# Last expert's first-half merge for all tiles at once, a tile-by-tile norm behind it, and late weights split in pieces

## The chip, the core and the metric

The kernel runs on one core of a Trainium2 chip. The metric is the device time of one launch in microseconds (us). Engines are named as the profile names them: PE (matrix products), DVE and ACT (elementwise work), POOL (a third elementwise engine that also issues some DMAs), SP (issues most DMAs).

## The reference

Two streams, a prompt of 256 tokens and a sample of 512, go separately through the same two layers of width 1024. Each layer adds an attention block and a mixture of 16 experts to the residual `x`; each expert chooses its own tokens, 2n/16 of a stream's n:

```python
def expert_choice_ffn(h, w_router, w_gate, w_up, w_down):
    ...
    aff = jax.nn.softmax(jnp.einsum('nd,de->ne', x, w_router).astype(jnp.float32), axis=-1)
    g, idx = lax.top_k(aff.T, cap)
    xe = x[idx]
    hid = jax.nn.silu(jnp.einsum('ecd,edf->ecf', xe, w_gate)) * jnp.einsum('ecd,edf->ecf', xe, w_up)
    ye = jnp.einsum('ecf,efd->ecd', hid, w_down) * g[..., None].astype(x.dtype)
    y = jnp.zeros_like(x).at[idx.reshape(-1)].add(ye.reshape(-1, d))
...
    for l in range(DEPTH):
        x = x + token_mixer(rmsnorm(x, norm1[l]), w_in[l], rpb[l], gain_na[l], gain_dil[l], w_out[l], slopes)
        x = x + expert_choice_ffn(rmsnorm(x, norm2[l]), w_router[l], w_gate[l], w_up[l], w_down[l])
    return rmsnorm(x, final_norm)
```

All values are fp32. `token_mixer` projects to q, k and v with `w_in`, attends, normalises each head and multiplies by `w_out`.

## The kernel before

The 768 tokens of both streams are six tiles of 128 rows. A product of two fp32 matrices is made as three products of rounded parts: every operand is split into `hi` (a rounding copy, on ACT) and `lo` (the operand minus `hi`, on DVE), and hi·hi, hi·lo and lo·hi are summed in PSUM. For the weights `Stream` does this: `prefetch` asks for a raw load, `convert` makes `hi` (L230) and `lo` (L231), and a load's turn comes as earlier buffers are freed. The experts of a layer use 192 loads of 128x2048 (1 MB), four for each of gate, up and down; the mixer's `w_in` comes in loads of 128x1024, two for each unit of its projection.

`experts` runs gate, up and down for one expert after another. The 96 chosen rows of an expert (64 of the sample, 32 of the prompt) are the stationary operand; a down product collects its two halves of 512 columns in the PSUM banks `av` and `o` (L366), then ACT scales them by the gate weight (L413) and POOL adds the rows to `xres` in DRAM by an indirect DMA (L414). The last expert, 15, is not scattered. The class `Ending` takes it into `x` by a product: `load` builds a 96x768 matrix `at` of ones and zeros (L539: six comparisons of an iota with the token numbers) and loads the residual as twelve pieces of 128x512 (L544); `scaled` makes hi and lo of one half of the expert's rows (L549, L550); `merge(t, b)` multiplies tile t's columns of `at` with half b (two products, L555), adds the result to `x` (L557) and sums squares (L558); `begin` multiplies the first half by the norm's gain (L562); `factor` makes 1/rms (L314 on DVE, then `pow` on POOL, L316); `normed` scales the begun half by it on ACT (L570) and makes the rest on DVE (L574).

This happens twice. At the seam between the layers, `Mixer.ended` runs `merge`, `factor` and `normed` per tile, stores `x` to `xres` (L701), `turn_rows` transposes the normed rows (L730; splits at L733, L734), and the first unit of `project`, "v", multiplies them with `w_in` (L827 to L829: 24 products a tile). At the end, `final` does the same without a projection and stores the output (L517). Between the first and the second half of the last down product, `merge(t, 0)` of tiles 0 to 3 is put in.

Each engine executes its instructions in program order. Around the seam that order comes from generators (`ended`, `turn_rows`, `project`), from which `Order` picks the next by estimated ready times of a `Clock`. `busy(n)` puts n dummy products of the identity with itself on PE.

## Time and profile before

| quantity | value |
|---|---|
| median of three runs | 2029.87 us (2029.84 to 2031.87) |
| profiled execution | 2031.46 us |
| its span in the trace | 2029.7 us |
| PE busy | 1974.6 us, 97% of the span |
| DVE, ACT, POOL busy | 78%, 67%, 11% |
| the seam in the trace | about 990 to 1044 us |
| the end in the trace | about 1997 us to the span's end |

Times in the trace count from the span's start. The profiled execution is 1.6 us above the median, and 1.76 us of it lie outside the span. A row of the timeline gives a start, a length, the engine, the line, what is written from what, and in brackets the idle time before it with what ended that; consecutive like instructions are one row. A matrix product shows its own length from start to end although the next begins before that: eleven products of 512 columns in 2.79 us are about 0.24 us each. "PEclk" is the granted clock as a share of the full 2.4 GHz; 0.50 is 1.2 GHz.

### The profile page before, as it was taken

How to read it: one execution, taken by the hardware profiler on the slowest of the kernel's cores; microseconds unless marked ns; L12 is line 12 of the kernel's file. 1: busy time of each engine (PE TensorE's matmuls, PEld its weight loads, DVE VectorE, ACT ScalarE, POOL GpSimd, SP SyncE). 2: the span in 40 equal slices, each digit the busy share in tenths (PEclk: the TensorE clock that was granted, in tenths of full speed). 3: DMA queues.
4: the chain of work that ended last, by engine and by line, in shares of the span. 5: the costliest groups of instructions: out<-in, count | busy, mean ns of one | idle time of the engine just before them, and what ended most of it. 6: DMA issues, size and time to landing. Idle time of an engine off the chain costs nothing.

```text
span 2029.7 us, 27925 instructions
## 1 busy us (share of the span) xinstructions
PE 1974.6 (97%) x10602; PEld 1551.6 (76%) x10602; DVE 1586.8 (78%) x1978; ACT 1349.9 (67%) x1743; POOL 217.3 (11%) x167
## 2 busy tenths in 40 slices
PE   7999999999999999999999999999899999999997
PEld 7899897886777777777689998978767777777774
DVE  5666667778888888888856666776788888888888
ACT  4666666437777777777646666654477777777775
POOL 3000000010101010101020000100110101011011
PEclk9999999999999999999999999999999999999999
DMA  6222124679999999999352212256799999999974
GB/s 229 85 79 81 58 77 174 234 261 367 376 394 375 398 380 396 380 389 351 121 189 74 97 58 77 69 184 253 292 354 392 387 382 398 377 398 376 398 275 143
DMA packets 96693, 526.67 MB, mean 259 GB/s; under 512 B 12112, under 2 KB 15440, under 8 KB 47408
## 3 DMA queue, kind: packets, MB, share of 16 engines
q1 hardware_dynamic: 82080, 489.20, 62.8%
q0 software_dynamic: 8992, 29.25, 5.7%
q10 hardware_dynamic: 5488, 6.45, 1.3%
q8 instruction: 83, 1.36, 0.3%
q14 instruction: 50, 0.41, 0.1%
HBM read 485.79 MB, written 32.77 MB: 255 GB/s over the span
## 4 chain that ended last, share of the span: by engine, by line
PE 89%; DVE 5%; ACT 3%; DMA 1%; issue 1%; POOL 0%; ACTq 0%; POOLq 0%; SPq 0%; DVEq 0%
PE pj L366 17%; PE s L366 17%; PE av L366 9%; PE o L366 8%; PE pj L1091 4%; PE pj L797 4%; PE pj L799 4%; PE pj L798 4%; PE tp L941 3%; PE pj L827 2%; PE pj L829 2%; PE pj L828 2%; PE tp L349 2%; PE s L1091 2%; PE s L908 2%; PE av L969 2%
## 5 line engine op out<-in xcount | busy, mean ns | idle before, releaser
L230 ACT ACTIVATE hi<-data 128x2048 fp32r<-128x2048 f32 (+1 forms) x170 | 289.5, 1703 | 61.3 <-PE s L366 24.6
L231 DVE TENSOR_TENSOR hi<-data,hi 128x2048 fp32r<-128x2048 f32 (+1 forms) x106 | 197.9, 1867 | 51.2 <-ACT hi L230 50.6
L366 PE MATMUL pj<-hi,parts 128*96 128x512 f32 x880 | 233.8, 393 | 2.8 <-DVE parts L352 2.3
L917 ACT ACTIVATE data<-data 128x256 f32<-128x256 f32 (+1 forms) x192 | 119.1, 621 | 155.5 <-DVE data L915 147.3
L366 PE MATMUL s<-turned_lo,parts 128*96 128x512 f32 x872 | 221.7, 393 | 0.0
L366 PEld LDWEIGHTS pj<-hi,parts 128*96 128x96 f32 x880 | 141.6, 161 | 64.8 <-DVE parts L352 3.2
L366 PEld LDWEIGHTS s<-turned_lo,parts 128*96 128x96 f32 x872 | 140.4, 161 | 60.7 <-DVE turned_lo L231 0.4
L797 PE MATMUL pj<-turned,hi 128*128 128x256 f32 (+1 forms) x512 | 178.4, 348 | 1.3 <-ACT heads L764 1.0
L366 PE MATMUL pj<-turned_lo,parts 128*96 128x512 f32 x656 | 178.9, 395 | 0.5 <-ACT parts L351 0.5
L230 ACT ACTIVATE hi<-heads 128x2048 fp32r<-128x2048 f32 x80 | 152.9, 1913 | 32.4 <-PE s L366 20.4
L799 PE MATMUL pj<-turned,hi 128*128 128x256 f32 (+1 forms) x512 | 172.5, 337 | 0.0
L798 PE MATMUL pj<-turned_lo,hi 128*128 128x256 f32 (+1 forms) x512 | 172.4, 337 | 0.0
L231 DVE TENSOR_TENSOR turned_lo<-data,hi 128x2048 fp32r<-128x2048 f32 x64 | 146.7, 2292 | 29.6 <-ACT hi L230 28.1
L366 PE MATMUL s<-hi,parts 128*96 128x512 f32 x664 | 169.0, 392 | 0.0
L231 DVE TENSOR_TENSOR turned_lo<-data,turned_lo 128x2048 fp32r<-128x2048 f32 (+1 forms) x68 | 151.4, 2226 | 16.8 <-ACT turned_lo L230 15.0
L414 POOL DMA_INDIRECT xres<-heads,iT x30 | 53.9, 1797 | 916.6 <-ACT heads L413 916.6
L230 ACT ACTIVATE turned_lo<-data 128x2048 fp32r<-128x2048 f32 (+1 forms) x68 | 127.0, 1868 | 27.8 <-PE pj L366 12.3
L366 PEld LDWEIGHTS s<-hi,parts 128*96 128x96 f32 x664 | 107.1, 161 | 46.3
L946 DVE TENSOR_TENSOR parts<-tp,parts 128x512 fp32r<-128x512 f32 (+2 forms) x160 | 99.6, 647 | 51.0 <-ACT parts L945 49.3
L366 PE MATMUL av<-hi,parts 128*96 128x512 f32 x400 | 134.9, 398 | 3.7 <-DVE hi L231 3.7
L366 PEld LDWEIGHTS pj<-turned_lo,parts 128*96 128x96 f32 x656 | 103.5, 162 | 42.3 <-ACT parts L351 0.9
L915 DVE CUSTOM_DVE_ANT_0 data<-s,data 128x512 f32<-128x512 f32 (+2 forms) x176 | 98.7, 579 | 28.8 <-PE s L909 27.1
(175 smaller groups left out, 4514.6 us busy)
## 6 DMA issues: line engine op xcount, KB each, us to landing
...
```

The costliest lines, as they stand in the source:

```text
L230: nc.scalar.activation(hi, w, AF.Copy)
L231: x = nc.vector.tensor_sub(lo, w, hi.bitcast(F32))
L366: nc.tensor.matmul(ps[b], y[:, k, :], a[:, o:o + 512], start=k == 0 and w == 0, stop=k == KT - 1 and w == 2)
L414: nc.gpsimd.indirect_dma_start(out=self.xres, out_offset=bass.IndirectOffsetOnAxis(ap=iT[:, e:e + 1], axis=0), in_=y, in_offset=None, comp ...
L797: nc.tensor.matmul(p, hi[:, k, :], hT[0][:, k, s], start=k == 0, stop=False)
L798: nc.tensor.matmul(p, hi[:, k, :], hT[1][:, k, s], start=False, stop=False)
L799: nc.tensor.matmul(p, lo[:, k, :], hT[0][:, k, s], start=False, stop=k == KT - 1)
L915: nc.vector.tensor_tensor_reduce(out=x[:, j, :w], in0=p[:, j, :w], in1=tab[:, o:o + w], scale=-1.0, scalar=3.0e38, op0=OP.add, op1=OP.min, ...
L917: nc.scalar.activation(x[:, j, :w], x[:, j, :w], AF.Exp, bias=m, scale=-1.0, accum_out=self.den[n][:, t, a:a + 1])
L941: nc.tensor.transpose(p[:, a * S + t * 128:a * S + (t + 1) * 128], w[:, o:o + 128], self.k.ident)
L946: nc.vector.tensor_sub(lo[:, c], p[:, c], hi[:, c].bitcast(F32))
L1091: nc.tensor.matmul(p, y[:, i], z[:, b * 512:(b + 1) * 512], start=i == 0 and w == 0, stop=i == len(ks) - 1 and w == 2)
```

## The change

The last three weight loads of each layer are converted in two pieces of 1024 columns. Expert 14's second half is scaled on DVE instead of ACT, and the conversions of these loads come right behind. The building of `at` moves from DVE to POOL. Between the halves of the last down product, the first half is multiplied for all six tiles (two use the `tp` banks), with adds of four tiles at the seam and all six at the end. The load of the first `w_in` part moves from POOL's DMA queue to SP's, and both parts are loaded ahead of the twelve `x` pieces and converted early, the second one's `lo` on POOL. `begin` covers two tiles instead of three at the seam, and six instead of four at the end, from tile 2 on by POOL. `ended` goes tile by tile in a fixed order, with dummy products between. The first layer's "v" unit waits for one weight part instead of two.

```diff
@@ class Stream, convert @@
+            pool = g in self.by_pool
+            n = size // self.pieces.get(g, 1)
+            for o in range(0, size, n):
+                c = slice(o, o + n)
...
-                nc.scalar.activation(hi, w, AF.Copy)
-                x = nc.vector.tensor_sub(lo, w, hi.bitcast(F32))
+                nc.scalar.activation(hi[:, c], w[:, c], AF.Copy)
+                x = (nc.gpsimd if pool else nc.vector).tensor_sub(lo[:, c], w[:, c], hi[:, c].bitcast(F32))
@@ experts @@
-            for b in range(2):
-                nc.scalar.activation(y[:, b * 512:(b + 1) * 512], dp[b], AF.Copy, scale=gT[:, e:e + 1])
+            nc.scalar.activation(y[:, :512], dp[0], AF.Copy, scale=gT[:, e:e + 1])
+            if e + 2 < EXPERTS:
+                nc.scalar.activation(y[:, 512:], dp[1], AF.Copy, scale=gT[:, e:e + 1])
+            else:
+                nc.vector.tensor_scalar_mul(y[:, 512:], dp[1], gT[:, e:e + 1])
+                ws.convert(stop - 2)
...
-        if m:
-            ws.prefetch(stop + 1, nc.gpsimd)
+        ws.prefetch(stop + 2)
         end.load()
         dp = acc("av", "o")
-        banks = {t: self.bank(("pj", "s")[t // 2]) for t in range(4)}
+        banks = {t: self.bank(("pj", "s", "tp")[t // 2]) for t in range(TILES)}
         for i in product(c, hT[last], dp, True):
             if i == 1:
                 end.scaled(0, dp[0])
+                ws.convert(min(stop + 1, len(ws.load)))
             if i == 2:
-                ws.prefetch(stop + 2)
-                for t in range(4):
-                    end.merge(t, 0, banks[t])
+                for t in range(TILES):
+                    end.multiply(t, 0, banks[t])
+                for t in range(4 if m else TILES):
+                    end.add(t, 0, banks[t])
+                    if t < 4:
+                        end.square(t, 0)
                 for t in range(end.early):
                     end.begin(t)
-                ws.convert(min(stop + 1, len(ws.load)))
         end.scaled(1, dp[1])
+        if m:
+            self.busy(BUSY[4])
+            end.add(4, 0, banks[4])
+            ws.convert(stop + 2)
+            end.rest = banks[5]
+        end.square(4, 0)
@@ expert_loads @@
+            if i >= len(src) - 3:
+                self.ws.pieces[n] = 2
@@ final @@
         def sums(t):
-            for b in range(t < 4, 2):
-                end.merge(t, b, self.bank(("pj", "s")[t % 2]))
+            end.merge(t, 1, self.bank(("pj", "s")[t % 2]))
@@ class Ending @@
-        self.early = 3 if m else 4
+        self.early = 2 if m else TILES
...
-            self.nc.vector.tensor_scalar(self.at[:, t * 128:(t + 1) * 128], self.k.iota, self.k.iL, -128.0 * t,
+            self.nc.gpsimd.tensor_scalar(self.at[:, t * 128:(t + 1) * 128], self.k.iota, self.k.iL, -128.0 * t,
...
-        self.nc.vector.tensor_mul(self.h[t][:, s], self.x[t][:, s], self.g[:, s])
+        (self.nc.vector if t < 2 else self.nc.gpsimd).tensor_mul(self.h[t][:, s], self.x[t][:, s], self.g[:, s])
@@ class Mixer, __init__ and ended @@
+        if l:
+            ws.by_pool.add(fi + 1)
...
+        merge(0)
+        busy(BUSY[5])
+        merge(1)
+        factor(0)
+        end.add(5, 0, end.rest)
+        merge(2)
+        busy(BUSY[6])
+        for t in range(TILES):
+            yield lambda: r_at[t] if self.turned >= t - 1 else NEVER
+            end.normed(t, rs[t])
+            if t == 0:
+                end.square(5, 0)
+            self.h_at[t] = clock.dve(512 if t < end.early else 1024, r_at[t])
+            if t + 1 < TILES:
+                factor(t + 1)
+            if t + 3 < TILES:
+                yield lambda: self.avail(("s", "pj")[(t + 3) // 2 % 2]) if self.turned > t else NEVER
+                merge(t + 3)
```

In the changed file the same lines have other numbers: L366 is L372, L555 is L575, L557 is L579, L562 is L592, L730 is L776, L827 is L882, L231 is L237, L549 and L550 are L569 and L570, and a dummy product is L311.

PE's program at the seam, before, from the last products of expert 15's first half (`av`) to the first product of the "v" unit (`pj<-hi,turned`); `parts` under L555 is the matrix `at`:

```order
L366 MATMUL av<-hi,parts 96x512 x13
L366 MATMUL o<-turned_lo,parts 96x512 x12
L555 MATMUL pj<-hi,parts 128x512 x4
L555 MATMUL s<-hi,parts 128x512 x4
...
L366 MATMUL o<-hi,parts 96x512
L555 MATMUL s<-hi,parts 128x512 x4
L555 MATMUL pj<-hi,parts 128x512 x4
L555 MATMUL s<-hi,parts 128x512 x4
L730 MATMUL tp<-ident,data 128x128 x8
L555 MATMUL s<-hi,parts 128x512 x4
L730 MATMUL tp<-ident,data 128x128 x8
L827 MATMUL pj<-hi,turned 128x256
```

The same place in the changed program, where `av<-ident` are the dummy products:

```order
L372 MATMUL av<-hi,parts 96x512 x13
L372 MATMUL o<-turned_lo,parts 96x512 x12
L575 MATMUL pj<-hi,parts 128x512 x4
L575 MATMUL s<-hi,parts 128x512 x4
L575 MATMUL tp<-hi,parts 128x512 x4
...
L311 MATMUL av<-ident 128x128 x5
L575 MATMUL s<-hi,parts 128x512 x2
L311 MATMUL av<-ident 128x128 x2
L575 MATMUL s<-hi,parts 128x512 x2
L575 MATMUL pj<-hi,parts 128x512 x2
L311 MATMUL av<-ident 128x128 x6
L776 MATMUL tp<-ident,data 128x128 x8
L575 MATMUL pj<-hi,parts 128x512 x2
L882 MATMUL pj<-hi,turned 128x256
```

All first-half merge products now stand between the halves of the down product; of the second-half ones eight stand ahead of the first "v" product instead of all, and the last two tiles' come between tiles of the "v" unit. The first "v" product follows one tile's transposes instead of two.

DVE's program at the seam, before, from expert 15's last split of hidden rows (L352) to the second scaled half:

```order
L352 TENSOR_TENSOR parts<-tp,parts 128x384 x2
L539 TENSOR_SCALAR parts<-iota,iL 96x128 x6
L231 TENSOR_TENSOR hi<-heads_3427,hi 128x2048
L231 TENSOR_TENSOR turned_lo<-heads_3711,turned_lo 128x2048
L231 TENSOR_TENSOR turned_lo<-turned,hi 128x2048
L550 SCALAR_TENSOR_TENSOR hi<-av,gT,hi 96x512
L557 TENSOR_TENSOR data<-data,pj 128x512 x2
L557 TENSOR_TENSOR data<-data,s 128x512 x2
L562 TENSOR_TENSOR data<-data 128x512 x3
L231 TENSOR_TENSOR hi<-data,hi 128x1024
L550 SCALAR_TENSOR_TENSOR hi<-o,gT,hi 96x512
```

And changed, where L422 is the scaling of expert 14's second half:

```order
L358 TENSOR_TENSOR parts<-tp,parts 128x384 x2
L422 TENSOR_SCALAR heads_3711<-o,gT 96x512
L237 TENSOR_TENSOR hi<-heads_3427,hi 128x1024 x2
L237 TENSOR_TENSOR turned_lo<-heads_3711,turned_lo 128x1024 x2
L237 TENSOR_TENSOR turned_lo<-turned,hi 128x1024 x2
L570 SCALAR_TENSOR_TENSOR hi<-av,gT,hi 96x512
L237 TENSOR_TENSOR hi<-data,hi 128x1024
L579 TENSOR_TENSOR data<-data,pj 128x512 x2
L579 TENSOR_TENSOR data<-data,s 128x512 x2
L592 TENSOR_TENSOR data<-data 128x512 x2
L570 SCALAR_TENSOR_TENSOR hi<-o,gT,hi 96x512
```

The six comparisons have left DVE, three conversions have become six, and the conversion of the first `w_in` part stands ahead of the adds instead of behind the `begin`s. On POOL, the end of the program changes from

```order
L339 DMA heads_11430<-table,iT 96x1024
L414 DMA xres<-heads_11430,iT 768x1024
L339 DMA heads_11430<-table,iT 96x1024
L414 DMA xres<-heads_11430,iT 768x1024 x2
L316 TENSOR_TENSOR data<-data,half 128x1 x6
```

to

```order
L345 DMA heads_11450<-table,iT 96x1024
L424 DMA xres<-heads_11450,iT 768x1024
L345 DMA heads_11450<-table,iT 96x1024
L424 DMA xres<-heads_11450,iT 768x1024 x2
L559 TENSOR_SCALAR parts<-iota,iL 96x128 x6
L592 TENSOR_TENSOR data<-data 128x512 x4
L322 TENSOR_TENSOR data<-data,half 128x1 x6
```

POOL now builds `at` and makes four of the begun halves (L592) ahead of the six `pow`s (L322). At the seam it builds `at` and makes the `lo` of the second `w_in` part ahead of them.

## Rows read from the trace of the kernel before

**Rows 1.** Page, part 1: busy time, share of the span and instructions of each engine

```profile
PE 1974.6 (97%) x10602; PEld 1551.6 (76%) x10602; DVE 1586.8 (78%) x1978; ACT 1349.9 (67%) x1743; POOL 217.3 (11%) x167
```

**Rows 2.** Stretches: length, PE busy (instructions), PEclk, DMA share, GB/s

```profile
994.00:997.00 3.00, 1.15 (x6) 0.96 1.02 180
997.00:1000.00 3.00, 3.00 (x9) 0.50 0.72 248
1008.00:1012.00 4.00, 2.36 (x6) 0.80 0.43 173
1020.00:1024.00 4.00, 3.35 (x16) 0.58 0.25 101
2001.00:2004.00 3.00, 2.42 (x11) 1.00 0.39 76
```

**Rows 3.** Timeline of PE, seam: start, length, operation, count, [idle, releaser]

```profile
995.90 4.29 PE L366 MATMUL av<-hi,parts 128*96 128x512 f32 x11 [1.85 <-DVE hi L231]
...
1002.85 1.09 PE L555 MATMUL pj<-hi,parts 96*128 96x512 f32 x4
...
1008.80 0.51 PE L555 MATMUL s<-hi,parts 96*128 96x512 f32 x1 [1.16 <-ACT hi L549]
...
1014.87 1.09 PE L730 MATMUL tp<-ident,data 128*128 128x128 f32 x8 [0.34 <-ACT data L570]
...
1020.65 1.97 PE L730 MATMUL tp<-ident,data 128*128 128x128 f32 x8 [3.05 <-DVE turned_lo L734]
...
1026.03 1.04 PE L730 MATMUL tp<-ident,data 128*128 128x128 f32 x8
...
1043.40 0.28 PE L829 MATMUL pj<-hi,turned_lo 128*128 128x256 f32 x1
```

**Rows 4.** Timeline of PE, end

```profile
2001.58 2.79 PE L366 MATMUL av<-hi,parts 128*96 128x512 f32 x11 [1.85 <-DVE hi L231]
```

**Rows 5.** Timeline of DVE, seam

```profile
993.55 2.29 DVE L231 TENSOR_TENSOR hi<-heads,hi 128x2048 fp32r<-128x2048 f32 x1 [2.39 <-ACT hi L230]
...
1003.52 1.28 DVE L557 TENSOR_TENSOR data<-data,pj 128x512 f32<-128x512 f32 x2 [1.83 <-PE pj L555]
...
1008.21 1.23 DVE L231 TENSOR_TENSOR hi<-data,hi 128x1024 fp32r<-128x1024 f32 x1 [0.41 <-ACT hi L230]
1009.35 0.74 DVE L550 SCALAR_TENSOR_TENSOR hi<-o,gT,hi 96x512 fp32r<-96x512 f32 x1
```

**Rows 6.** Timeline of ACT, seam

```profile
1004.24 0.63 ACT L558 ACTIVATE data<-data 128x512 f32<-128x512 f32 x1 [3.33 <-DVE data L557]
...
1008.08 0.67 ACT L549 ACTIVATE hi<-o,gT 96x512 fp32r<-96x512 f32 x1
```

**Rows 7.** Operations of POOL in the whole program: busy us, mean ns

```profile
L785 POOL MEMSET heads<- 64x768 f32 x8 | 5.9, 737 | 0.4
...
L1015 POOL TENSOR_TENSOR data<-data,half 128x8 f32<-128x8 f32 x16 | 27.9, 1744 | 356.9 <-DVE data L1012 356.9
...
L1015 POOL TENSOR_TENSOR data<-data,half 128x4 f32<-128x4 f32 x16 | 16.2, 1011 | 270.7 <-DVE data L1012 234.3 <-issue 36.4
```

**Rows 8.** Timeline of POOL, end

```profile
2015.69 0.57 POOL L316 TENSOR_TENSOR data<-data,half 128x1 f32<-128x1 f32 x1 [16.58 <-DVE data L314]
2016.44 1.02 POOL L316 TENSOR_TENSOR data<-data,half 128x1 f32<-128x1 f32 x1 [0.18 <-DVE data L314]
```

**Rows 9.** Timeline of DVE, end

```profile
2010.05 2.49 DVE L562 TENSOR_TENSOR data<-data 128x512 f32<-128x512 f32 x4
...
2024.56 1.29 DVE L574 SCALAR_TENSOR_TENSOR data<-data 128x1024 f32<-128x1024 f32 x1 [0.44 <-POOL data L316]
```

**Rows 10.** DMA issues from 2005.0 to 2005.6 (KB, us to landing), traffic from 2024 to 2026

```profile
data<-xres SPq DMA_DIRECT2D x2, 256.0 KB, 5.1
...
DMA packets 212, 0.80 MB, mean 401 GB/s; under 512 B 16, under 2 KB 16, under 8 KB 212
```

**Rows 11.** Timeline of DVE, kernel start

```profile
18.59 1.28 DVE L734 TENSOR_TENSOR turned_lo<-tp,turned 128x512 fp32r<-128x512 f32 x2
```

87 lines of the change are left out of this document (48 added, 39 removed).

## Prediction

> **What bounds the kernel now.** I read the page's engine shares first: PE is busy for 97% of the span, DVE for 78, ACT for 67, POOL for 11 [rows 1]. So time can only be won where PE stands still or runs at the lower clock, and the order of the programs differs at three places alone: the kernel's start, the seam between the layers, and the end. Then the windows of the seam [rows 2]: from 994 to 997 PE works 1.15 of 3 us, from 997 to 1000 it is busy throughout but at a granted clock of 0.50 (1.2 GHz), from 1008 to 1012 it works 2.36 of 4 us, and from 1020 to 1024 the clock is 0.58. Then PE's timeline, with what ended each wait [rows 3]: 1.85 us for DVE's conversion of an expert weight (995.90), 1.16 for ACT's hi of expert 15's second half (1008.80), then merges in small pieces, and 3.05 us before tile 1's transposes (1020.65), which wait for DVE's lo of tile 0. From 1026.03 on PE has no wait to speak of until the "v" unit ends at 1043.40 + 0.28 = 1043.7. The seam is therefore bound by chains through ACT and DVE, and a gain there is a gain of the whole.
>
> **The change part by part.**
>
> *Weights in pieces.* DVE stands 2.39 us until ACT has made hi of a whole load (at 993.55) [rows 5], and needs 2.2 us for a load; a piece of 1024 columns takes 1.14 (1008.21 to 1009.35) [rows 5]. With the comparisons gone from DVE, the scaling of expert 14's half there, and hi of a piece ready after half the time, six pieces run from about 991.7 to 991.7 + 6 x 1.14 = 998.5, each ahead of its products, so the 1.85 goes. It is followed by eleven products in 4.29 us [rows 3]; the same eleven behind the same wait at the end take 2.79 [rows 4], where the clock is 1.00 [rows 2]. So the slow stretch, 1.5 us, goes as well. Expert 15's first half then has its lo at 998.5 + 0.75 = 999.2, about when PE is through the first twelve products of the second half.
>
> *All six merges between the halves.* Twelve products instead of eight. Four take 0.93 from start to start (1.09 with the last tail, at 1002.85) [rows 3], twelve 2.8: 999.2 to 1002.0, and the second half of the down product, 2.8 us, ends at 1004.8, against 1007.6 before. Its adds go to DVE beside it and wait for nobody.
>
> *The second half's hi and lo.* Before, ACT had four squares ahead, from 1004.24 on, and began hi at 1008.08 [rows 6]; DVE had three begun halves and a conversion ahead, and lo was ready at 1009.35 + 0.74 = 1010.1 [rows 5]. Now DVE has two begun halves ahead and the w_in conversion is earlier: hi 1005.0 to 1005.65, lo at 1006.3, 3.8 us earlier.
>
> *Tile by tile.* From 1006.3: tile 0's second product and add until 1007.7, then on ACT the squares of tiles 4, 0, 1, 2, 0.755 each [rows 6], ahead of tile 0's scaling. That gives 1011.3 for tile 0's transposes, where they begin at 1014.87 now [rows 3]. Thereafter PE is short of work until tile 1: transposes 2.0 us at the lower clock (as in row 1020.65), 1.9 for two splits, 24 "v" products of which half run at 0.21 us and half at 0.12 (the distance of starts at 0.58 and at full clock), 4.0; then transposes 0.87, tile 1's products 2.9 and tile 2's transposes 0.87: 1023.9. What is left is 4 x 24 x 0.12 + 3 x 0.87 = 14.1 us, so the unit ends at 1038.0. Before, five tiles of products and four of transposes were left at 1026.03: 17.9, so 1043.9, which the trace confirms. The gain is 5.9 us. It holds 1.2 us of loss because I let the clock fall once, behind the idle time from 1009.4 to 1011.3 that the thirteen dummies fill only in part. Each dummy is short, and none delays a product that is ready, so I cost them at nothing; if they did stand ahead of ready work, they would cost their own length.
>
> *The comparisons on POOL.* POOL is free from the last scatter to the first `pow`, so their own time is covered. The cost is where they run beside DVE's conversions, which read two operands from SBUF. What the trace shows is the other direction: a POOL operation of one column takes 0.57 alone and 1.02 when a DVE operation with two operands runs [rows 8], 0.45 more. If DVE waits as POOL does, six comparisons cost six times at most 0.4 = 2.4; if not, 0. I take 1.0, the middle rounded down, as pieces have slack ahead of PE. The Trainium skill, page "SBUF — State Buffer", section "SBUF: two separate sides", says that VectorE and GpSimd share one pair of ports as an exclusive lock, so that whichever starts first blocks the other for its whole instruction; the trace agrees for POOL being blocked, and no row shows DVE blocked. By that rule the lock alone would take 2.4 instead of 1.0; this is the second rival.
>
> *The second w_in part's lo on POOL.* No row has a subtraction of this width there. A fill of 768 columns takes 737 ns [rows 7], so 1024 columns 0.98 us, the lower bound; the slope of the `pow`s, (1744 - 1011) / 4 = 183 ns a column [rows 7], is an upper bound far out of reach of a plain subtraction. I take twice the fill, 1.9 us, since it reads two operands. It begins at 1006.6 and ends at 1008.5, and tile 0's `pow` is asked for at 1008.65, so it is covered; with more than 2.05 us every further us is on the path. The Trainium skill, page "GPSIMD Engine Reference", section 3.1, gives 4497 ns for an addition of 2048 fp32 columns on GpSimd against 2293 on VectorE; an estimate by it is 2.25 us for 1024, and the sum would be 0.2 lower.
>
> *The end.* The residual's last first-half piece, issued at 2005.2, lands 5.1 us later [rows 10], and it waits for the last scatter, which now shares DVE's time; I give that 0.5, between 0 and 1.0. So 2010.8, add 0.6, two begun halves of 0.62 [rows 9], lo of the second half 0.75: 2013.4 against 2012.51 + 0.75 = 2013.26 now, a loss of 0.15. (2010.05 + 2.49 is where the four begun halves end [rows 9].) POOL's four begun halves take 1.2 us each at twice DVE's time and are done before their tiles' scaling; beside DVE I give 0.6 of loss. Then DVE needs 12.6 us until 2024.56 + 1.29 = 2025.85 [rows 9], and 10.3 after the change: two adds of 0.6 and two halves of 0.55 less. Half of this is lost again, because six stores of 524 KB at 401 GB/s [rows 10] take 1.3 us each while rows come each 0.6 to 0.75 us: gain 1.3 of 2.3. Net 1.3 - 0.15 - 0.6 = 0.5.
>
> *The start.* The split of tile 0's "v" now stands ahead of tile 1's two subtractions, which begin at 18.59 [rows 11]; those end some 0.3 later. I count -0.3, between 0 and -0.7.
>
> The sum is 5.9 - 1.0 + 0.5 - 0.3 = 5.1 us. On the profiled execution, 2031.46, that is 2026.4; this execution lies 1.6 above the median of the three runs, and nothing that changes is known to lie in these 1.6, so I take the 5.1 off the median: 2024.8.
>
> **The rivals.**
>
> *First: the dummies hold the clock and POOL blocks nobody.* For it: the wait at the end before 2001.58 is as long as that at 995.90, and the clock stayed at 1.00 there. Against: the idle time at 1009 to 1011 is not covered by the dummies' length. The 1.2, the 1.0 and the 0.6 come back: 7.9 us, 2022.0.
>
> *Second: the lock works both ways.* For it: the 0.45 of [rows 8]. Against: the conversions have slack ahead of PE. 1.4 more for the comparisons and 0.6 more for the begun halves at the end: gain 3.1, 2026.8, which is no change that can be told.
>
> *Third: POOL is far slower than DVE at plain operations on wide rows.* Its `lo` of 1024 columns stands ahead of all `pow`s of the seam, and four begun halves stand ahead of those of the end. If POOL needs m times DVE's time, the seam loses 1.14m - 2.05, the end 2.48m - 7.2, and 5.1 is used up at m = 4. At m = 6, 4.8 and 7.7 are lost: 2029.87 - 5.1 + 12.5 = 2037.3. For it: 183 ns a column for `pow`; against: the fill at 0.96 ns a column.
>
> *Fourth: the time is given back behind the seam.* The third w_in load is asked for behind tile 5's store, which comes no earlier than before (some 1023.4), while its user is now 6 us earlier. It should land at about 1028 and is wanted at 1037; if loads behind it are late instead, or the attention's order waits for something that did not move, the gain is gone: 2029.9.
>
> **How the numbers follow.** The forecast has 0.43 with a range of its own from 2023.3 to 2026.3 (comparisons 0 to 2.4, scatter and start at their bounds), the first rival 0.20, the second 0.21, the third 0.10, the fourth 0.06. A difference of 0.2%, 4.1 us, is about what a measurement of this kernel can tell from none: below 2025.8 is faster, above 2033.9 slower. Faster is nearly all of the forecast (0.40) and the first rival, 0.60; the second and fourth and the rest of the forecast are the same, 0.30; the third is slower, 0.10. The range reaches from 2021.6, just under the first rival, to 2030.0, which takes in the fourth; about 0.18 lies outside.
>
> **What would show it.** Right: no wait of about 1.85 before expert 15's last first-half products at the seam, and the eleven products in 2.8 us; tile 0's transposes near 1011; the "v" unit's last product at 1038 and everything behind it 5 to 6 us earlier by the trace; POOL's subtraction under 2.05 us. Wrong: DVE's pieces longer than 1.2 us beside POOL's comparisons; the wait for the conversions still there; `pow` of tile 0 late because POOL is still subtracting; the last store ending as late after the last down product as before.

## The result, and the profile after

The changed kernel takes 2045.02 us (median of four runs, 2042.86 to 2045.93) against 2030.87 for the kernel before on the same chip: a ratio of 1.0062 [1.0049, 1.0074], so 0.62% slower. I had predicted 2024.8, faster. The profiled execution of after is 2045.93 us with a span of 2043.8, 14.1 more than before's 2029.7. PE's busy time on the page grew by 9.2 of these:

```profile
PE 1983.8 (97%) x10628; PEld 1559.1 (76%) x10628; DVE 1584.5 (78%) x1970; ACT 1350.8 (66%) x1748; POOL 244.4 (12%) x183
```

A stage table says where they arose. A scatter is POOL's indirect DMA that adds an expert's rows to `xres`; two of them cut the span in three: that of layer 0's expert 13 (it begins at 957.37 in before, 957.77 in after) and the first of layer 1 (1513.00 and 1519.04). The numbers are by how much each stretch is longer than in before's trace.

| stretch | after |
|---|---|
| start: up to the scatter of expert 13 | +0.40 |
| seam: from there to the first scatter of layer 1 | +5.64 |
| end: from there to the span's end | +8.06 |

I then read the engine that I had thought free. POOL's timeline of after, seam (992.95 to 1016.27) and end (2004.27 and 2022.90); columns as in [rows 3]:

```profile
992.95 9.14 POOL L424 DMA_INDIRECT xres<-heads,iT  x1 [33.35 <-ACT hi L236]
1001.66 4.63 POOL L559 TENSOR_SCALAR parts<-iota,iL 96x128 fp32r<-96x128 f32 x6
1016.27 2.37 POOL L237 TENSOR_TENSOR hi<-data,hi 128x1024 fp32r<-128x1024 f32 x1 [9.98 <-ACT hi L236]
...
2004.27 7.34 POOL L424 DMA_INDIRECT xres<-heads,iT  x1 [33.36 <-ACT hi L236]
...
2022.90 5.84 POOL L592 TENSOR_TENSOR data<-data 128x512 f32<-128x512 f32 x4 [7.08 <-DVE data L579]
```

L424 is the scatter of expert 14, the last before the expert that is merged. It holds POOL for 9.14 us at the seam and 7.34 at the end. In before it takes 1.44 and 1.43; the other 28 of either trace take 1.69 to 1.88. The two of before:

```profile
991.99 1.44 POOL L414 DMA_INDIRECT xres<-heads,iT  x1 [32.79 <-ACT heads L413]
...
1997.67 1.43 POOL L414 DMA_INDIRECT xres<-heads,iT  x1 [32.81 <-ACT heads L413]
```

DVE of after in that time:

```profile
991.43 0.75 DVE L422 TENSOR_SCALAR heads<-o,gT 96x512 f32<-96x512 f32 x1 [1.05 <-PE o L372]
992.10 2.35 DVE L237 TENSOR_TENSOR hi<-heads,hi 128x1024 fp32r<-128x1024 f32 x2
...
996.63 2.35 DVE L237 TENSOR_TENSOR turned_lo<-turned,hi 128x1024 fp32r<-128x1024 f32 x2
998.90 0.74 DVE L570 SCALAR_TENSOR_TENSOR hi<-av,gT,hi 96x512 fp32r<-96x512 f32 x1
999.57 1.21 DVE L237 TENSOR_TENSOR hi<-data,hi 128x1024 fp32r<-128x1024 f32 x1
1009.53 1.34 DVE L579 TENSOR_TENSOR data<-data,pj 128x512 f32<-128x512 f32 x2 [8.75 <-DMA data<-xres]
...
2007.95 2.35 DVE L237 TENSOR_TENSOR turned_lo<-turned,hi 128x1024 fp32r<-128x1024 f32 x2
2010.22 0.74 DVE L570 SCALAR_TENSOR_TENSOR hi<-av,gT,hi 96x512 fp32r<-96x512 f32 x1
2019.10 1.33 DVE L579 TENSOR_TENSOR data<-data,pj 128x512 f32<-128x512 f32 x2 [8.14 <-DMA data<-xres]
```

From 991.43 to 1000.78 DVE has no idle time: the scaling on 96 partitions (L422), six pieces (L237), lo of expert 15's first half (L570), a w_in part. The scatter falls into this stream and ends at 1002.09, 1.31 us after the last conversion. At the end of the kernel the last piece ends at 2010.30, and the scatter again 1.31 later, at 2011.61; L570, which follows that piece without a rest until 2010.96, does not hold it longer. In before DVE waits for ACT's hi in just this place, from 991.16 to 993.55 [rows 5], and the scatter goes out in that wait, from 991.99 to 993.43. Is the transfer slow, or does it not begin? The windows of after (columns as in [rows 2]) show no traffic in seven of the nine microseconds:

```profile
993.00:1000.00 7.00, 6.74 (x30) 1.00 0.00 0
1000.00:1004.00 4.00, 1.07 (x3) 0.89 0.38 45
1016.00:1020.00 4.00, 4.00 (x14) 0.50 0.89 347
```

It does not begin. All that stands behind it is then late. The comparisons are behind it on POOL and begin at 1001.66. The residual's loads wait until its rows are in DRAM, and SP asks for them at 1006.10 where before it did at 997.46 (before, then after):

```profile
997.46 6.57 SPq L544 DMA_DIRECT2D data<-xres  x12
...
1006.10 7.25 SPq L564 DMA_DIRECT2D data<-xres  x12
```

DVE waits 8.75 us for these loads (1009.53), ACT's hi of the second half comes behind DVE's adds, and PE, which had been brought ahead of before's times, stands still twice:

```profile
993.78 3.17 PE L372 MATMUL av<-hi,parts 128*96 128x512 f32 x13
...
1002.93 1.92 PE L575 MATMUL pj<-hi,parts 96*128 96x512 f32 x4 [3.20 <-POOL parts L559]
...
1015.30 1.58 PE L575 MATMUL s<-hi,parts 96*128 96x512 f32 x2 [3.86 <-ACT hi L569]
...
1022.10 1.09 PE L776 MATMUL tp<-ident,data 128*128 128x128 f32 x8 [0.90 <-ACT data L600]
```

The thirteen products of 993.78 run without the 1.85 wait of [rows 3] and at full clock. Then PE waits 3.20 for the comparisons and 3.86 for the second half's hi; the clock is 0.50 from 1016 to 1020, and tile 0's transposes come at 1022.10 instead of 1014.87 [rows 3].

### The profile page after: what moved, and what is told of

The parts are those of the page before. It is cut to its first block, busy times and chain, and to the rows that moved or that the text cites. A ratio compares the mean times of both kernels' runs of the same rounds, so it can differ in the third digit from the quotient of the medians.

```text
span 2043.8 us, 28007 instructions
## 1 busy us (share of the span) xinstructions
PE 1983.8 (97%) x10628; PEld 1559.1 (76%) x10628; DVE 1584.5 (78%) x1970; ACT 1350.8 (66%) x1748; POOL 244.4 (12%) x183
## 3 DMA queue, kind: packets, MB, share of 16 engines
q8 instruction: 84, 1.38, 0.3%
## 4 chain that ended last, share of the span: by engine, by line
PE 87%; DVE 5%; ACT 4%; DMA 3%; issue 1%; ACTq 0%; POOL 0%; SPq 0%; DVEq 0%; POOLq 0%
PE pj L372 17%; PE s L372 17%; PE o L372 8%; PE av L372 8%; PE pj L1146 4%; PE pj L843 3%; PE pj L845 3%; PE pj L844 3%; PE tp L996 3%; PE pj L882 2%; PE pj L884 2%; PE pj L883 2%; PE tp L355 2%; PE s L1146 2%; PE av L1024 2%; PE s L963 2%
## 5 line engine op out<-in xcount | busy, mean ns | idle before, releaser
L372 PE MATMUL pj<-hi,parts 128*96 128x512 f32 x880 | 233.8, 393 | 2.8 <-DVE parts L358 2.3
L237 DVE TENSOR_TENSOR hi<-data,hi 128x2048 fp32r<-128x2048 f32 (+1 forms) x105 | 196.7, 1873 | 50.1 <-ACT hi L236 49.5
L372 PE MATMUL s<-turned_lo,parts 128*96 128x512 f32 x872 | 221.7, 393 | 0.0
L372 PEld LDWEIGHTS pj<-hi,parts 128*96 128x96 f32 x880 | 141.6, 161 | 64.8 <-DVE parts L358 3.2
L372 PEld LDWEIGHTS s<-turned_lo,parts 128*96 128x96 f32 x872 | 140.4, 161 | 60.8 <-DVE turned_lo L237 0.4
L372 PE MATMUL pj<-turned_lo,parts 128*96 128x512 f32 x656 | 178.9, 395 | 0.5 <-ACT parts L357 0.5
L424 POOL DMA_INDIRECT xres<-heads,iT x30 | 67.6, 2254 | 917.6 <-ACT heads L420 850.8
L236 ACT ACTIVATE hi<-heads 128x2048 fp32r<-128x2048 f32 (+1 forms) x82 | 153.3, 1872 | 33.6 <-PE s L372 20.4
L237 DVE TENSOR_TENSOR turned_lo<-data,hi 128x2048 fp32r<-128x2048 f32 x64 | 146.7, 2293 | 29.6 <-ACT hi L236 28.1
L372 PE MATMUL s<-hi,parts 128*96 128x512 f32 x664 | 169.0, 392 | 0.0
L237 DVE TENSOR_TENSOR turned_lo<-data,turned_lo 128x2048 fp32r<-128x2048 f32 (+1 forms) x68 | 151.4, 2227 | 16.7 <-ACT turned_lo L236 15.0
L372 PEld LDWEIGHTS s<-hi,parts 128*96 128x96 f32 x664 | 107.1, 161 | 46.3
L372 PEld LDWEIGHTS pj<-turned_lo,parts 128*96 128x96 f32 x656 | 103.5, 162 | 42.3 <-ACT parts L357 0.9
L372 PE MATMUL av<-hi,parts 128*96 128x512 f32 x400 | 132.9, 393 | 0.0
```

What stands on the lines that cost most here:

```text
L236: nc.scalar.activation(hi[:, c], w[:, c], AF.Copy)
L237: x = (nc.gpsimd if pool else nc.vector).tensor_sub(lo[:, c], w[:, c], hi[:, c].bitcast(F32))
L372: nc.tensor.matmul(ps[b], y[:, k, :], a[:, o:o + 512], start=k == 0 and w == 0, stop=k == KT - 1 and w == 2)
L424: nc.gpsimd.indirect_dma_start(out=self.xres, out_offset=bass.IndirectOffsetOnAxis(ap=iT[:, e:e + 1], axis=0), in_=y, in_offset=None, comp ...
```

## The experiments

Where an edit is shown, it is made to the changed kernel unless it says otherwise. "Seam" and "end" are the rows of the stage table; "start" is -0.2 to +0.7 in all but e_act (+1.9). Ratios are to the kernel before on the same chip. best1 and e_nodum run the same program at the end and differ there by 1.2, so less than that in one row of this table is not an effect.

| kernel | scatters, us | seam | end | ratio [95%] |
|---|---|---|---|---|
| after | 9.14, 7.34 | +5.64 | +8.06 | 1.0062 [1.0049, 1.0074] |
| e_wait | 1.43, 1.43 | -0.97 | +0.93 | 1.0002 [.9993, 1.0011] |
| e_act | 1.43, 1.43 | -2.87 | +0.89 | .9999 [.9990, 1.0009] |
| e_only | 1.44, 1.43 | +0.17 | +1.69 | 1.0004 [.9995, 1.0014] |
| e_whole | 1.43, 1.43 | -0.34 | +2.63 | 1.0002 [.9992, 1.0011] |
| e_pieces | 1.44, 1.43 | -1.02 | +0.79 | .9994 [.9985, 1.0003] |
| e_act_at | 1.43, 1.43 | -3.32 | +1.82 | .9989 [.9980, .9998] |
| best1 | 1.44, 1.44 | -3.85 | +1.38 | .9982 [.9973, .9991] |
| e_nodum | 1.44, 1.44 | -2.09 | +0.21 | .9989 [.9980, .9998] |
| e_fill | 9.15, 7.36 | +3.87 | +7.80 | 1.0063 [1.0048, 1.0079] |
| e_fill128 | 9.15, 7.35 | +4.69 | +8.42 | 1.0065 [1.0048, 1.0082] |
| e_mul | 9.13, 7.34 | +6.79 | +8.47 | 1.0066 [1.0049, 1.0082] |
| e_rows | 1.66, 1.66 | -2.84 | +2.73 | 1.0000 [.9991, 1.0010] |
| best2 | 1.67, 1.67 | -3.35 | +1.42 | .9991 [.9982, 1.0000] |

**Does DVE's stream hold the scatter?** In e_wait the first piece on DVE waits until the scatter is out (a fill behind it on POOL releases it); in e_act the scaling goes back to ACT.

```diff
@@ e_wait @@
-                ws.convert(stop - 2)
             nc.gpsimd.indirect_dma_start(...)
+            if e + 2 == EXPERTS:
+                ws.behind = nc.gpsimd.memset(self.mark, 0.0)
+                ws.convert(stop - 2)
@@ e_act @@
-            nc.scalar.activation(y[:, :512], dp[0], AF.Copy, scale=gT[:, e:e + 1])
-            if e + 2 < EXPERTS:
-                nc.scalar.activation(y[:, 512:], dp[1], AF.Copy, scale=gT[:, e:e + 1])
-            else:
-                nc.vector.tensor_scalar_mul(y[:, 512:], dp[1], gT[:, e:e + 1])
-                ws.convert(stop - 2)
+            for b in range(2):
+                nc.scalar.activation(y[:, b * 512:(b + 1) * 512], dp[b], AF.Copy, scale=gT[:, e:e + 1])
```

> The changed kernel with one edit: expert 14's scatter is issued first, and VectorE's first late conversion waits until POOL has issued it. Theory 1 (in the changed kernel POOL cannot finish issuing the scatter while VectorE subtracts back to back with two SBUF operands): both late scatters take 1.4 to 1.9 us instead of 9.1 and 7.3, VectorE's pieces begin 2 to 2.5 us later, the residual loads at the seam are asked for 6 to 8 us earlier, and the time falls by 10 to 16 us to 2028 to 2035. Theory 2 (the scatter is slow because the DMA engines carry more traffic when it is issued): the scatters stay at 7 to 9 us and the time rises by about 4 to 2047 to 2050. Theory 3 (the loss is the slow building of the one-hot matrix on POOL, 4.6 us where VectorE took 1.3): the scatters may be short, but the time stays above 2041.

> The changed kernel with that one part undone: expert 14's second half is scaled on ScalarE again, and the late conversions come in their old place. VectorE then has nothing to do for about 1 us behind the scatter's start. Theory 1: if that gap is enough the scatters take 1.4 to 2.5 us and the time falls to 2028 to 2036; if an issue that is not through is held by what follows, it stays near 8 us and the time near 2044. Theory 2: about 8 us and 2044 in any case. Theory 3: short scatters, but a time above 2041.

In both the scatter takes 1.43 us and the 0.62% are gone. POOL and DVE of e_wait:

```profile
993.28 1.43 POOL L423 DMA_INDIRECT xres<-heads,iT  x1 [33.35 <-ACT hi L236]
...
994.32 11.27 POOL L561 TENSOR_SCALAR parts<-iota,iL 96x128 fp32r<-96x128 f32 x6
```

```profile
994.79 2.36 DVE L237 TENSOR_TENSOR hi<-heads,hi 128x1024 fp32r<-128x1024 f32 x2 [2.28 <-POOL mark L427]
```

A wait of 2.28 us put into DVE's program saves the kernel some 12 us. The trace of e_act has a wait of 2.71 on DVE in the same place, for ACT's hi, which now stands behind the scaling. Both have another cost in view: the six comparisons, 4.63 us in after where POOL runs them with DVE at rest, take 11.27 beside the pieces.

**Which part closes the rest?** e_only puts the scaling and the early conversion into the kernel before; e_whole takes the change with whole loads; e_pieces puts the pieces alone into the kernel before.

```diff
@@ e_only, to the kernel before @@
+            if e + 2 < EXPERTS:
+                nc.scalar.activation(y[:, 512:], dp[1], AF.Copy, scale=gT[:, e:e + 1])
+            else:
+                nc.vector.tensor_scalar_mul(y[:, 512:], dp[1], gT[:, e:e + 1])
+                ws.convert(stop - 2)
@@ e_whole @@
-                self.ws.pieces[n] = 2
+                self.ws.pieces[n] = 1
@@ e_pieces, to the kernel before, with convert's loop over pieces @@
+            if i >= len(src) - 3:
+                self.ws.pieces[n] = 2
```

> The kernel before with one part of the change alone: expert 14's second half is scaled on VectorE and the next conversions follow right behind it (whole loads, nothing moved to POOL). Theory 1: with VectorE busy from the scatter's start on, the last scatter of each layer takes 6 to 9 us instead of 1.44, the residual loads come 5 to 7 us later, and the time rises by 5 to 15 us to 2035 to 2045. Theory 2 and theory 3: the scatter keeps 1.4 to 1.9 us and the time stays within 2 us of 2030.

> The changed kernel with the last three loads converted whole again (2048 columns in one instruction); all else as changed. Theory 1: VectorE still subtracts without a rest behind the scaling, now with three instructions of 2.2 us instead of six of 1.14, so the scatters stay at 6 to 9 us and the time at 2041 to 2047. Rival (it is the short pieces, whose many small instructions keep POOL out): the scatters take 2 to 4 us and the time falls to 2030 to 2036.

> The kernel before with one part of the change alone: the last three weight loads of each layer are converted in two pieces each. Scaling stays on ScalarE, so the scatters should take 1.4 us. Prediction's first term: the wait of 1.85 us ahead of the last first-half products falls to 0 to 0.9 at the seam and at the end, and the slow stretch of clock behind it goes; 1.5 to 4 us faster than the kernel before. Rival (the gain is given back because the adds then wait for the residual's loads): within 1 us of the kernel before.

The first two expectations missed: no scatter is held in any of the three. DVE of e_whole shows why:

```profile
991.23 0.75 DVE L422 TENSOR_SCALAR heads<-o,gT 96x512 f32<-96x512 f32 x1 [1.04 <-PE o L372]
993.18 2.42 DVE L237 TENSOR_TENSOR hi<-heads,hi 128x2048 fp32r<-128x2048 f32 x1 [1.20 <-ACT hi L236]
```

With whole loads DVE still rests 1.20 us behind the scaling, for ACT's hi (e_only has the same 1.20), and the scatter at 992.75 goes out in it. Neither edit costs anything by itself; together they fill DVE's program without a gap. e_pieces also says what the pieces alone are worth: .9994, no change that can be told. The wait of 1.85 goes and comes back at the next link, the second half's hi, 2.97 where it was 1.16 [rows 3]:

```profile
1008.36 0.49 PE L562 MATMUL s<-hi,parts 96*128 96x512 f32 x1 [2.97 <-ACT hi L556]
```

**What in the stream holds it?** Five small kernels, each profiled once, leave out the encoder. In each stretch an instruction on DVE releases a scatter of 96 rows on POOL while DVE goes on with a stream of its own; what was measured is the length of the scatter's instruction.

```python
def segment(steps, by):
    ...
    done = [f() for f in steps]        # on DVE, in this order
    order(tc, scatter(), done[by])     # POOL waits for one of them
...
    ([ptr(128), p7], 0), ([ptr(96), p7], 0), ...   # m_rows: scaling, then seven pieces
```

> Only the disputed cost, without the encoder: a scatter of 96 rows is issued by POOL with VectorE idle, beside ten subtractions of 128x1024 from SBUF, beside five of 128x2048, beside ten one-operand operations, beside sixteen subtractions with one operand in PSUM, and beside eight subtractions with short pauses between; then six comparisons and two subtractions on POOL, each alone and beside ten subtractions on VectorE. Theory 1: alone 1.4 us; beside the two-operand streams until the stream ends, 10 to 12 us; beside one SBUF operand 1.4 to 2; with pauses 2 to 5. Theory 2: every scatter alike, 1.4 to 2 us. For POOL's own operations: comparisons 0.77 us each alone; if the block works both ways, VectorE's subtractions beside them grow from 1.14 us by the length of what blocks them, otherwise they stay.

> Only the disputed cost again, without the encoder, now as close to the changed kernel as can be: a scaling of 96x512 on VectorE releases the scatter, and behind it VectorE subtracts pieces of 1024 columns. In m_lock the scatter got through at the first end of a VectorE instruction (2.2 us); in the changed kernel it did not. Seven stretches: seven pieces with ScalarE's hi and rounded results; the same without ScalarE; unrounded results; unrounded and released by a tiny fill; ScalarE's hi, rounded and released by the tiny fill; twelve pieces like the first; twelve with a pause behind the fourth. Theory 1a (what VectorE writes or waits for decides): 8 us or more with ScalarE's hi or with rounded results, 2.2 in the others. Theory 1b (when the scatter starts against VectorE's instructions decides): 8 us or more in every stretch released by the scaling, 2.2 where the fill releases it. Theory 1c (something else of the large kernel is needed, such as PE's traffic): about 2.2 us in all seven. If it is held until VectorE rests, twelve pieces hold it for 13 us or more, and the pause lets it through after five.

In m_lock a tiny fill releases it, and ten subtractions of 1024 columns do not hold it. With DVE at rest, beside those ten, and beside five of 2048 columns:

```profile
84.98 1.55 POOL L81 DMA_INDIRECT xres<-y,iT  x1 [84.15 <-DVE go L100]
...
86.96 2.19 POOL L81 DMA_INDIRECT xres<-y,iT  x1 [0.39 <-DVE go L100]
...
98.35 3.21 POOL L81 DMA_INDIRECT xres<-y,iT  x1 [9.17 <-DVE go L100]
```

So it gets through at the first boundary between two instructions of DVE or near it: 2.19 beside ones of 1.14 us, 3.21 beside ones of 2.2. Beside one-operand instructions it took 1.76, beside subtractions with one operand in PSUM 1.43, and with short pauses between the subtractions 2.15. By this my theory of an unbroken stream would have fallen. m_pieces copies the kernel's order, the scaling on 96 partitions and then seven pieces; in order: that; released by a fill with no scaling; twelve pieces; twelve with a rest behind the fourth.

```profile
75.61 9.05 POOL L54 DMA_INDIRECT xres<-y,iT  x1 [74.78 <-DVE y L80]
...
113.35 2.17 POOL L54 DMA_INDIRECT xres<-y,iT  x1 [0.50 <-DVE go L82]
...
130.08 14.64 POOL L54 DMA_INDIRECT xres<-y,iT  x1 [6.42 <-DVE y L80]
...
149.87 5.56 POOL L54 DMA_INDIRECT xres<-y,iT  x1 [5.11 <-DVE y L80]
```

9.05 with the scaling ahead of it, 2.17 without; twelve pieces hold it for 14.64, and a rest behind the fourth lets it out at 5.56. With or without ACT's work at the side, and for rounded or unrounded pieces, it was the same (8.97 each).

> The disputed cost by itself, third time: in m_pieces the scatter was held until VectorE rested (9.0 us for seven pieces, 14.6 for twelve) when a scaling of 96x512 released it, and got through at the first end of a piece (2.2 us) when a tiny fill did, though it began equally late (0.35 us) in the first piece. Eight stretches: scaling, fill, pieces, released by the scaling; the same, released by the fill; fill, scaling, pieces, released by the fill; a first piece releases, seven more follow; a one-operand operation of 1024 columns releases; scaling and fourteen pieces of 512; scaling and four of 2048; scaling, two pieces, a fill, five pieces. Theory 1d (VectorE takes the port for its next instruction before the last one ends wherever the next has long been queued; a fill, whose own time is shorter than what the next one needs to be ready, opens it): 2 to 3 us where a fill stands straight ahead of the pieces (first two stretches), 3.5 to 4.5 in the last, and 9 or more in the other five. Theory 1e (what releases the scatter decides): 2.2 in the second and third, 9 in the others.

> The disputed cost by itself, fourth time. In m_prime the scatter got through at the first end of a piece behind a fill, behind a piece, or behind a one-operand operation with a constant factor (2.2 us), and was held until VectorE rested wherever the scaling stood ahead, with or without a fill between. The scaling differs from those in three things: it writes the scatter's source y, it reads its factor from a column in SBUF, and it reads PSUM. Eight stretches, each with six or seven pieces behind: scaling by a column, PSUM to another tile z; scaling by a constant, PSUM to y; fill of y; scaling by a column, SBUF to z; a piece, then ScalarE scales into y and releases, pieces go on; scaling by a column into y, then twelve one-operand operations of 512; scaling by a constant, PSUM to z; scaling by a column to z, a piece releases, six more. Theory 1f (the factor read from a column): 9 us in the first, fourth and eighth, 2.2 in the second, third, fifth and seventh. Theory 1g (VectorE wrote y): 9 in the second and third, 2.2 in the first, fourth, fifth, seventh and eighth. Theory 1h (VectorE read PSUM): 9 in the first, second and seventh, 2.2 in the third, fourth and fifth. The sixth: 1.4 to 2 if it is two operands that hold the port.

These tried what it is about the scaling. Behind a piece or a one-operand instruction of 1024 columns, both on 128 partitions, the scatter passes (2.16 each). It is not which instruction releases the scatter (a fill behind the scaling: 8.96; a piece behind it: 7.83, which is again to the stream's end), not the order of a fill (8.97), not the size of the pieces (9.45 for 512 columns, 9.83 for 2048), not a fill in the midst of the pieces (8.98). It is not that the scaling reads PSUM (8.97 from SBUF), that its factor is a column (8.96 for a constant), or that it writes the rows to be scattered (8.97 into another tile; a fill of them, 8.91). Scaled on ACT behind a piece, it passes (2.09). Nor need the stream read two operands: twelve one-operand instructions of 512 columns behind the scaling hold it to their end (5.04). One stretch of m_src does not count, because its scatter began late for another reason (4.68).

> The disputed cost by itself, fifth time. Theories 1f, 1g and 1h fell: the scatter was held behind a scaling by a column or a constant, from PSUM or SBUF, into y or z, and behind a fill of y. All of these have 96 partitions; all operations behind which it got through have 128 partitions or one. After a first scatter with VectorE idle, eight stretches with seven pieces behind: scaling of 128 partitions, of 96, of 64; a fill of one column of 96 partitions; of 128; scaling of 96 and then a fill of 128; fill of 96 and then a fill of 128; scaling of 32. Theory 1i (an instruction on 96 partitions ahead makes VectorE keep POOL out until it rests): 9 us in the second, fourth and perhaps the sixth and seventh, 2.2 in the first, third, fifth and eighth. Theory 1j (any number of partitions other than 1 and 128): 9 in the third and eighth too. Theory 1k (the first operation's length of 0.4 to 0.75 us and 512 columns decide): 9 in the first, second, third and eighth, 2.2 in the fourth and fifth.

What is left is the count of partitions. m_rows has the scaling on 128, then on 96 partitions, then a fill of one column on 96 in its place, and the scaling on 32:

```profile
95.60 2.22 POOL L54 DMA_INDIRECT xres<-y,iT  x1 [94.77 <-DVE o L61]
...
100.78 8.97 POOL L54 DMA_INDIRECT xres<-y,iT  x1 [2.92 <-DVE z L68]
...
120.25 2.15 POOL L54 DMA_INDIRECT xres<-y,iT  x1 [0.41 <-DVE many L65]
...
155.00 8.97 POOL L54 DMA_INDIRECT xres<-y,iT  x1 [6.41 <-DVE z L68]
```

128 partitions: 2.22; 96, 64 and 32: 8.97, 8.96, 8.97; one column on 96: 2.15. A planned first scatter with DVE at rest did not come about, and the 128 stretch began late; e_rows repeats it in the kernel. Nor need the scaling come first in DVE's stream. Here is that of m_rows on 32 partitions; it has no idle time before it, because it follows the pieces of the stretch before:

```profile
153.99 0.73 DVE L68 TENSOR_SCALAR z<-bank,gT 32x512 f32<-32x512 f32 x1
```

What counts is that it stands in the unbroken stream just ahead of the scatter; how far ahead it may stand was not tested beyond one instruction between.

**In the kernel.** e_fill and e_fill128 put a fill of one column, on 1 and on 128 partitions, between the scaling and the pieces; e_mul writes the scaling as a product of two tensors, still on 96 partitions; e_rows scales 128 partitions (rows 96 to 127 of the bank are zeroed by DVE earlier).

```diff
@@ e_fill, e_fill128 @@
                 nc.vector.tensor_scalar_mul(y[:, 512:], dp[1], gT[:, e:e + 1])
+                nc.vector.memset(self.fill, 0.0)
@@ e_mul @@
-                nc.vector.tensor_scalar_mul(y[:, 512:], dp[1], gT[:, e:e + 1])
+                nc.vector.tensor_mul(y[:, 512:], dp[1], gT[:, e:e + 1].to_broadcast([CAP, 512]))
@@ e_rows @@
-                nc.vector.tensor_scalar_mul(y[:, 512:], dp[1], gT[:, e:e + 1])
+                nc.vector.tensor_scalar_mul(y128[:, 512:], whole[1], self.gT128[:, e:e + 1])
```

> The changed kernel with one added instruction: a fill of one element on VectorE between the scaling of expert 14's second half and the pieces, which nobody waits for. Theory 1d: the scatters get through at the first end of a piece, 2 to 3 us instead of 9.1 and 7.3, the residual loads come 6 us earlier, and the time falls by 11 to 15 us to 2030 to 2034. Theory 1e: the scaling still releases the scatter, so nothing changes (2043 to 2047).

> The changed kernel with expert 14's second half on VectorE still, but made as a product of two tensors (the gate weight broadcast) instead of a scaling by a column. Theory 1f: the scatters get through at the first end of a piece, 2 to 3 us, and the time falls by 11 to 15 us to 2030 to 2034. Theory 1g and 1h: as the changed kernel, scatters 7 to 9 us, 2043 to 2047.

> The changed kernel with a fill of one column on 128 partitions on VectorE between the scaling of 96 partitions and the pieces (e_fill had a fill of one element there and changed nothing). Theory 1i with the last instruction ahead of the pieces deciding: scatters 2 to 3 us and 2030 to 2034 us. If any instruction of 96 partitions ahead in the unbroken stream decides: scatters 7 to 9 us, 2042 to 2047.

> The changed kernel with expert 14's second half scaled on VectorE on all 128 partitions instead of 96 (the 32 further rows are filled with zeros beforehand and used by nobody); all else as changed, pieces right behind. In m_rows the scatter was held until VectorE rested behind a scaling of 32, 64 or 96 partitions and got through at the first end of an instruction behind one of 128. Theory 1i/1j (an instruction of 512 columns on fewer than 128 partitions at the head of the stream closes it): both scatters 2 to 3 us, residual loads 6 us earlier, 2030 to 2035. Rival (in the kernel any stream that starts with the scaling holds the scatter): 7 to 9 us, 2043 to 2047.

The fills and the product change nothing (9.13 to 9.15). With 128 partitions DVE's stream has the same length and no rest either, and the scatter passes:

```profile
992.48 1.66 POOL L432 DMA_INDIRECT xres<-heads,iT  x1 [33.37 <-ACT hi L236]
993.70 9.44 POOL L567 TENSOR_SCALAR parts<-iota,iL 96x128 fp32r<-96x128 f32 x6
...
2008.58 5.85 POOL L600 TENSOR_TENSOR data<-data 128x512 f32<-128x512 f32 x4 [4.31 <-DVE data L587]
```

```profile
990.95 0.75 DVE L430 TENSOR_SCALAR heads<-o,gT 128x512 f32<-128x512 f32 x1 [1.03 <-PE o L374]
991.62 2.35 DVE L237 TENSOR_TENSOR hi<-heads,hi 128x1024 fp32r<-128x1024 f32 x2
...
2004.90 1.33 DVE L587 TENSOR_TENSOR data<-data,pj 128x512 f32<-128x512 f32 x2 [2.63 <-DMA data<-xres]
...
2010.39 2.91 DVE L600 TENSOR_TENSOR data<-data 128x512 f32<-128x512 f32 x2
```

The ratio falls from 1.0062 to 1.0000, 12.6 us of 2032, and the spans by 14.3 (2043.8 to 2029.5). That is the whole loss, shown by the count of partitions in one instruction (and the zeroing of rows that it needs). Why an instruction on fewer partitions keeps the issue out for the rest of the stream is open.

**What the other edits are worth.** e_act_at is e_act with the comparisons back on DVE. best1 adds before's code of the start and the end (four merges between the halves there, all begun halves on DVE; the pieces stay); best2 is best1 with e_rows' scaling on DVE; e_nodum is best1 without the dummies of the seam.

```diff
@@ e_act_at, best1, e_nodum: as e_act, and @@
-            self.nc.gpsimd.tensor_scalar(self.at[:, t * 128:(t + 1) * 128], self.k.iota, self.k.iL, -128.0 * t,
+            self.nc.vector.tensor_scalar(self.at[:, t * 128:(t + 1) * 128], self.k.iota, self.k.iL, -128.0 * t,
@@ best1, e_nodum @@
-        self.early = 2 if m else TILES
+        self.early = 2 if m else 4
...
-        (self.nc.vector if t < 2 else self.nc.gpsimd).tensor_mul(self.h[t][:, s], self.x[t][:, s], self.g[:, s])
+        self.nc.vector.tensor_mul(self.h[t][:, s], self.x[t][:, s], self.g[:, s])
@@ e_nodum @@
-            self.busy(BUSY[4])
...
-        busy(BUSY[5])
...
-        busy(BUSY[6])
```

> As e_act (ScalarE scales expert 14's second half again), and the six comparisons are back on VectorE, in its idle time ahead of the conversions. Theory 1 with the comparisons as a second, smaller loss: POOL's 10.5 us beside VectorE become 1.3 on VectorE, which hides them; the conversions keep 1.14 instead of 1.19; the first merges no longer wait for the matrix: 0.5 to 1.5 us faster than e_act, 2030 to 2031.5 where before stands at 2031.9. Rival (the comparisons cost nothing on POOL): as e_act within 0.3.

> As e_act_at, and the kernel's start and end are those of the kernel before (four merges between the halves at the end, four begun halves on VectorE); the seam keeps the pieces, the merges of all six tiles between the halves, and the norm tile by tile. Theory: the end of e_act lost 0.9 us and the start 0.4, the seam won 2.9; so this one takes 0.8 to 1.5 less than e_act_at and 2.5 to 4.5 us less than the kernel before. Rival (the seam's gain is given back later): within 1 us of the kernel before.

> As best1 without the thirteen dummy products at the seam. Theory of the prediction (they keep the clock of TensorE up and delay nothing): the granted clock at the seam falls to 0.5 for 3 to 7 us, and the time rises by 1 to 3 us over best1. Rival (they are too short to matter): within 0.5 us of best1, clock at the seam unchanged.

> best1 with the scaling of expert 14's second half back on VectorE, on 128 partitions, and the pieces right behind it. If the scatter gets through at the first end of a piece: it ends 1.2 to 1.5 us later than in best1, the pieces begin 0.4 earlier; the residual's loads bound the adds, so 0.5 to 2 us slower than best1. If it is held: 12 us slower than best1.

best1 is faster than both kernels, and faster than before by 0.18% (2029.11 against 2033.37 on the same chip, .9982 [.9973, .9991]). It keeps what the change did for the seam: tile 0's transposes at 1012.88, and the "v" unit's last copy out of PSUM by ACT at 1040.52, against 1044.08 in before.

```profile
1009.56 1.50 PE L311 MATMUL av<-ident 128*128 128x128 f32 x12
1012.88 1.09 PE L771 MATMUL tp<-ident,data 128*128 128x128 f32 x8 [1.82 <-ACT data L595]
```

In best1 the clock stays up over the wait of 1.82 behind the dummies of 1009.56. The windows of best1 and then of e_nodum:

```profile
1008.00:1012.00 4.00, 3.06 (x21) 1.00 0.99 389
1012.00:1016.00 4.00, 2.90 (x20) 1.00 0.52 210
```

```profile
1008.00:1012.00 4.00, 1.10 (x4) 0.57 0.95 375
1012.00:1016.00 4.00, 3.49 (x15) 0.50 0.40 162
```

Full clock with them, 0.57 and 0.50 without, and the seam is 1.8 us longer by the traces (-3.85 and -2.09). But the ratios, .9982 and .9989, do not separate the two, and both spans are 2027.6. Nor is it shown that the dummies always suffice. e_rows has the same dummies and the same wait of 1.82 behind them (1013.44), and its clock falls:

```profile
1012.00:1016.00 4.00, 2.56 (x14) 0.83 0.74 303
1016.00:1020.00 4.00, 4.00 (x27) 0.74 0.34 136
```

best2's scaling on DVE gains nothing over ACT's.

## Why the prediction was wrong, step by step

*What bounds the kernel: half right.* The seam is bound by chains, as I said, and every microsecond there came through in the total. But I ranked the engines by busy share and dropped POOL at 11%. Its last scatter is at the head of three chains (the residual's loads, the comparisons, and through DVE's adds the second half).

*The scatter: the step that failed.* At the end I wrote that the load "waits for the last scatter, which now shares DVE's time; I give that 0.5, between 0 and 1.0". It took 5.9 more (7.34 against 1.43). For the seam I had no term at all: "POOL is free from the last scatter to the first `pow`". There it took 7.7 more (9.14 against 1.44). The two stretches cost 8.5 and 5.3 us (after less e_rows: 5.64 + 2.84, 8.06 - 2.73), 13.8 of the 14.3 by which their spans differ. The 0.5 names no row; it is about the price of one POOL operation beside one DVE operation, the 0.45 of [rows 8]. The runs showed a wait for the end of a stream of conversions, whose length the change itself made: it closed the 2.39 of [rows 5], which I had counted as idle time to be won. That rest was when the scatter went out.

*Weights in pieces: right.* Six pieces from 992.10 to 998.98 (forecast 991.7 to 998.5), no 1.85, products at full clock. e_pieces adds that the 1.85 counts only if the link behind it moves too.

*Tile by tile: right in kind, too large.* Where the scatter is quick, the "v" unit ends 3.6 us earlier (best1, 1040.52 against 1044.08), not 5.9. Tile 0's transposes come at 1012.88 and not at 1011.3: 1.6 of the missing 2.3. DVE's lo of the second half ends at 1007.8 there, forecast 1006.3, because DVE waits 1.02 for the residual and then 0.55 for ACT. The other 0.7 lies behind the first tile, where two errors partly cancel. My sum left out the merges of tiles 4 and 5, which stand between tiles of the "v" unit (0.55 each), and PE's waits there (0.22, 0.82, 0.59 and 0.44 in best1). Against that, the clock did not fall in best1. I called that loss 1.2, but the terms of my sum hold about 2.0 of it (2.0 instead of 1.09 for the transposes, twelve products at 0.21 instead of 0.12), and with it the first rival's 7.9 would be 8.7.

*Comparisons on POOL: wrong side.* I looked for what they cost DVE and took 1.0. The pieces lengthen by a quarter of a microsecond in all (e_rows: 2.51 and 2.44 for two against 2.35). It is POOL that is slowed: 9.44 for six, so PE waits 0.67 for them in e_rows. e_act and e_act_at do not separate the price by their ratios.

*w_in's lo on POOL: nearly covered.* It takes 2.37, where I took 1.9 and had 2.05 of slack, and tile 0's `pow` begins 0.2 behind the instruction that asks for it (best1). The estimate by the Trainium skill, page "GPSIMD Engine Reference", section 3.1, was nearer with 2.25, and the trace agrees with its ratio (2.37 to 1.2 on DVE).

*The end: wrong without the scatter too.* e_rows loses 2.73 where I had forecast a gain of 0.5. DVE waits 2.63 for the residual's first piece (2004.90), where in before it waits 1.06 for PE, and two begun halves take 2.91 beside POOL's (2010.39), 1.66 more than alone [rows 9] where I gave 0.6. Here the second rival was right: POOL blocks DVE. Taken one by one, the two engines' products alternate: DVE's first ends at 2011.63, 0.55 after POOL's second (2011.08), and POOL's third at 2012.75, 1.12 after that. The rule that I quoted for it, from the Trainium skill, page "SBUF — State Buffer", section "SBUF: two separate sides", is borne out in this direction. From the second half's lo on the forecast held: DVE needs 10.3 us (2013.95 to 2024.24, forecast 10.3), and 1.4 of the 2.3 so won are lost behind it (forecast 1.0).

*The start* stays within what the traces differ by from run to run (-0.2 to +1.9).

*The rivals.* The first was right on the clock in best1 and wrong on POOL. The third, a POOL many times slower than DVE, fell: twice DVE's time for the subtraction and for a begun half that DVE does not block (1.27 against 0.62), where it needed four times. The fourth fell too: the 3.6 won at 1040.52 in best1 are still there at the next scatter (-3.85). No rival had the scatter. Without the hold the sum is -0.1 - 2.8 + 2.7 = -0.2 (e_rows), so no change: the forecast's 5.1 was 4.9 too much by its ordinary terms, and 14 more by the scatter, put at 0.5 at the end and at nothing at the seam.
